# A two-layer gated decoder trunk on one core: more weight units in seven products, softmax every three steps, the residual in device memory, ScalarE's own silu and gelu

## The chip, the cores and the metric

One core of one Trainium2 chip runs the whole program. The metric is the device time of one execution in microseconds, lower is better. The engines are named as in the profile: PE is TensorE (PEld its weight loads), DVE is VectorE, ACT is ScalarE, POOL is GpSimd, SP is SyncE, which here only issues transfers.

## The reference, cut

The input x is 256 positions of 2048 channels in float32. Two layers run one after the other; each is:

```python
h = rms_norm(x, mix_norm[l])
q, k, v, uv, gate_logits = jnp.split(h @ w_in[l], cuts, axis=-1)     # 1024 | 256 | 256 | 2048 | 4096 columns
q = apply_rope(rms_norm(q, q_norm[l])); k = apply_rope(rms_norm(k, k_norm[l]))
branch_a = sliding_window_attention(q, k, v, sinks[l]) @ w_attn_branch[l]        # window 128, blocks of 128, sinks
branch_b = chunked_sgu(gelu(uv), w_spatial[l], b_spatial[l], ...) @ w_sgu_branch[l]
gates = sigmoid(gate_logits)
x = x + (gates[..., :2048] * branch_a + gates[..., 2048:] * branch_b) @ w_out[l]
h2 = rms_norm(x, ffn_norm[l])
x = x + (silu(h2 @ w_gate[l]) * (h2 @ w_up[l])) @ w_down[l]                     # 5632 hidden channels
```

All weights and results are float32.

## The kernel before

**Products.** A float32 product is made of three matmuls in a rounded format (fp32r): the weight's high part against the activation's high part, the low part against the high, the high against the low (lines L368, L369, L370). Each weight tile is read from device memory (`raw`, 1 MB a transfer, a ring of four, SP's queue). ScalarE rounds it into `whi` (L241, six buffers, 128x1024), VectorE subtracts to get `wlo` (L249, five buffers). One such pair is a *part*. The activations are transposed, scaled and split once into `uh` and `ul`; 512 input channels of them are a *unit*.

**Jobs and units in seven.** A *job* is one product with up to 1024 output columns: a list of units, run one after the other by `run`. A plain unit has four parts of 12 matmuls. A job's first `m` units are instead made as a Strassen product of 2x2 blocks: seven parts of 6 matmuls in the order `PRODUCTS`, where four of the seven weight tiles are differences of others, made by VectorE (L224, into `sum` or in place in `raw`), and four of the activations' blocks are sums kept in `sh` and `sl` (L491, L494, L479). With m = 2 each of the seven steps does both units. `M_FFN`, `M_GATE` and the like say how many units of a job are in seven. A job in seven takes five accumulators, and ends its Strassen part with copies by ScalarE (L402, L405) and two adds by VectorE (L408).

**Order of the work.** All five engines run in the order in which the code is recorded. `stream.next` records, ahead of part i on TensorE, the high part up to i+5, the low part up to i+4 and the weight differences a little further ahead (`SUM_AHEAD`). A low part can start only when TensorE has finished the part five before, since it takes that part's buffer. Side work is put at *slots*: a plain part counts one slot, a part in seven half a slot; `after(n, fn)` records fn n slots later. `calm(n, fn)` counts plain parts alone. `evicting` takes the results of a job out of the accumulators: those of the second column half are spread over the next job, later if the next job is in seven (`T1_LATE`, `THEN_LATE`).

**Side work.** `transposed` transposes a tile by VectorE (`blk`, L454), 16 small transfers of GpSimd's queue (`tt`), a scaling and a split by ScalarE, and a subtraction by VectorE. `residual` adds a product to x, which lies in on-chip memory (`xs`), and transposes the sum for the next norm. In `Attention`, each of eight groups of heads and rows goes through `scores` (two PSUM tiles `psc`), one step later `masked`, then `exps`, `inverse`, six steps after its scores `weights` (one or two transposes `ppt`), nine after them `values` (`po`) and ten after them `weighted` (`att`, L870); groups start every `Q_STEP` steps. `psc`, `ppt`, `po` and the spatial unit's `psg` share the three PSUM buffers of the pool `ps_at`. Silu, gelu and sigmoid are built from tanh with VectorE's help, so that one activation table serves the whole program.

## Time and profile before

| | |
|---|---|
| median of 3 runs | 2468.36 us (2466.8 to 2468.55) |
| the profiled execution | 2468.03 us, its span 2466.3 us |
| busy: PE, DVE, ACT, POOL | 2455.4, 1887.3, 1373.3, 470.7 us |
| granted TensorE clock | 1.000 |
| read from device memory | 475.27 MB, 194 GB/s over the span |

A group's row in the profile gives line, engine, operation, output and inputs by the program's names, shapes and count; after the first bar the busy time and the mean of one in ns; after the second the engine's idle time just before them, and who ended most of it. A row of a timeline gives start, length, engine, line and operation, with the idle time before it in brackets. Matmuls are pipelined: one is 0.39 us long, but the next starts before it ends. VectorE's and ScalarE's operations overlap a little, too.

### The profile page before, as it was taken

How to read it: one execution, taken by the hardware profiler on the slowest of the kernel's cores; microseconds unless marked ns; L12 is line 12 of the kernel's file. 1: busy time of each engine (PE TensorE's matmuls, PEld its weight loads, DVE VectorE, ACT ScalarE, POOL GpSimd, SP SyncE). 2: the span in 40 equal slices, each digit the busy share in tenths (PEclk: the TensorE clock that was granted, in tenths of full speed). 3: DMA queues.
4: the chain of work that ended last, by engine and by line, in shares of the span. 5: the costliest groups of instructions: out<-in, count | busy, mean ns of one | idle time of the engine just before them, and what ended most of it. 6: DMA issues, size and time to landing. Idle time of an engine off the chain costs nothing.

```text
span 2466.3 us, 30726 instructions
## 1 busy us (share of the span) xinstructions
PE 2455.4 (100%) x11046; PEld 2029.3 (82%) x11046; DVE 1887.3 (77%) x2107; ACT 1373.3 (56%) x1688; POOL 470.7 (19%) x903
## 2 busy tenths in 40 slices
PE   9999999999999999999999999999999999999999
PEld 8888888888888888888888888888888888888887
DVE  6797675797977687778867976757878776977696
ACT  6565455476655555555655554544756555655554
POOL 1411300541220022002235022014402200220020
PEclk9999999999999999999999999999999999999999
DMA  8644656766565557566766456566756665665564
GB/s 295 221 156 159 213 172 221 221 217 228 204 220 190 206 204 239 171 229 199 230 235 216 156 169 207 189 195 201 252 187 239 205 208 202 206 223 189 203 205 153
DMA packets 162730, 507.73 MB, mean 206 GB/s; under 512 B 22912, under 2 KB 25584, under 8 KB 162576
## 3 DMA queue, kind: packets, MB, share of 16 engines
q1 hardware_dynamic: 134512, 477.05, 57.7%
q0 software_dynamic: 27744, 28.44, 3.8%
q8 instruction: 86, 1.41, 0.2%
q14 instruction: 68, 0.56, 0.1%
q10 hardware_dynamic: 320, 0.27, 0.0%
HBM read 475.27 MB, written 2.10 MB: 194 GB/s over the span
## 4 chain that ended last, share of the span: by engine, by line
PE 98%; DVE 1%; DMA 0%; ACT 0%; issue 0%; POOL 0%; DVEq 0%; ACTq 0%; POOLq 0%
PE acc L368 32%; PE acc L369 32%; PE acc L370 32%; PE po L864 1%; PE psc L822 1%; DMA tt<-blk 0%; PE ppt L853 0%; PE psg L949 0%; DVE wlo L249 0%; PE pt L533 0%; PE pwarm L346 0%; POOL tt L460 0%; DVE sums L491 0%; DVE blk L454 0%; DVE ul L519 0%
## 5 line engine op out<-in xcount | busy, mean ns | idle before, releaser
L249 DVE TENSOR_TENSOR wlo<-raw,whi 128x1024 fp32r<-128x1024 f32 (+1 forms) x940 | 1132.8, 1218 | 486.1 <-PE acc L369 398.1
L241 ACT ACTIVATE whi<-raw 128x1024 fp32r<-128x1024 f32 (+1 forms) x940 | 983.4, 1057 | 823.1 <-PE acc L370 746.3
L368 PE MATMUL acc<-whi,uh 128*128 128x512 f32 x3164 | 1240.0, 392 | 2.2 <-DVE gate L1043 1.5
L370 PE MATMUL acc<-whi,ul 128*128 128x512 f32 x3164 | 1233.0, 390 | 0.5 <-DVE ul L561 0.5
L369 PE MATMUL acc<-wlo,uh 128*128 128x512 f32 x3164 | 1232.8, 390 | 0.7 <-DVE wlo L249 0.7
L460 POOL DMA_DIRECT2D tt<-blk x800 | 392.2, 497 | 1715.4 <-DVE blk L454 959.7
L368 PEld LDWEIGHTS acc<-whi,uh 128*128 128x128 f32 x3164 | 594.3, 188 | 130.6 <-ACT acc L402 2.7
L370 PEld LDWEIGHTS acc<-whi,ul 128*128 128x128 f32 x3164 | 594.2, 188 | 124.9 <-DVE ul L561 1.0
L369 PEld LDWEIGHTS acc<-wlo,uh 128*128 128x128 f32 x3164 | 594.5, 188 | 122.1 <-DVE wlo L249 1.4
L368 PE MATMUL acc<-whi,sh 128*128 128x512 f32 x336 | 131.0, 390 | 0.8 <-ACT acc L402 0.8
L370 PE MATMUL acc<-whi,sl 128*128 128x512 f32 x336 | 130.9, 390 | 0.0
L369 PE MATMUL acc<-wlo,sh 128*128 128x512 f32 x336 | 130.9, 389 | 0.0
L241 ACT ACTIVATE whi<-sum 128x1024 fp32r<-128x1024 f32 x84 | 89.0, 1059 | 72.7 <-PE acc L370 56.7
L249 DVE TENSOR_TENSOR wlo<-sum,whi 128x1024 fp32r<-128x1024 f32 x84 | 102.6, 1222 | 13.4 <-ACT whi L241 11.0
L402 ACT ACTIVATE acc<-acc 128x512 f32<-128x512 f32 x126 | 74.4, 590 | 21.7 <-PE acc L370 19.8
L368 PEld LDWEIGHTS acc<-whi,sh 128*128 128x128 f32 x336 | 63.1, 188 | 14.3 <-ACT acc L402 1.2
L370 PEld LDWEIGHTS acc<-whi,sl 128*128 128x128 f32 x336 | 63.1, 188 | 13.1
L369 PEld LDWEIGHTS acc<-wlo,sh 128*128 128x128 f32 x336 | 63.1, 188 | 13.0
L561 DVE TENSOR_TENSOR ul<-tt,uh 128x1024 fp32r<-128x1024 f32 x38 | 46.5, 1223 | 34.1 <-ACT uh L558 27.3
L558 ACT ACTIVATE uh<-tt 128x1024 fp32r<-128x1024 f32 x38 | 40.2, 1057 | 43.9 <-DMA tt<-blk 41.3
L408 DVE TENSOR_TENSOR acc<-acc,p 128x512 f32<-128x512 f32 x84 | 54.2, 691 | 0.0
L224 DVE TENSOR_TENSOR sum<-raw,raw 128x1024 f32<-128x1024 f32 x42 | 51.5, 1226 | 1.4
(131 smaller groups left out, 1053.1 us busy)
## 6 DMA issues: line engine op xcount, KB each, us to landing
raw<-in_w_in_dram SPq DMA_DIRECT2D x112, 1024.0 KB, 5.1
raw<-in_w_down_dram SPq DMA_DIRECT2D x88, 1024.0 KB, 6.3
raw<-in_w_gate_dram SPq DMA_DIRECT2D x80, 1024.0 KB, 5.8
raw<-in_w_up_dram SPq DMA_DIRECT2D x80, 1024.0 KB, 5.1
raw<-in_w_out_dram SPq DMA_DIRECT2D x32, 1024.0 KB, 6.7
tt<-blk POOLq DMA_DIRECT2D x800, 32.0 KB, 5.1
raw<-in_w_attn_branch_dram SPq DMA_DIRECT2D x16, 1024.0 KB, 6.4
raw<-in_w_sgu_branch_dram SPq DMA_DIRECT2D x16, 1024.0 KB, 5.6
```

The lines of the kernel that those rows point to most:

```text
L224: nc.vector.tensor_tensor(out=self.raw(dst), in0=self.raw(total[0]), in1=self.raw(total[1]), op=ALU.subtract)
L241: nc.scalar.activation(hi[:, k, :], raw[:, k, :], AF.Copy)
L249: nc.vector.tensor_tensor(out=lo[:, k, :], in0=raw[:, k, :], in1=hi[:, k, :].bitcast(F32), op=ALU.subtract)
L368: nc.tensor.matmul(ps, a, hi, start=first, stop=False, skip_group_check=True)
L369: nc.tensor.matmul(ps, a, lo, start=False, stop=False, skip_group_check=True)
L370: nc.tensor.matmul(ps, b, hi, start=False, stop=last, skip_group_check=True)
L402: nc.scalar.activation({"11": x, "t2": e, "t3": y}[name], a, AF.Copy)
L408: nc.vector.tensor_tensor(out=d, in0=d, in1=fifth, op=ALU.add)
L460: nc.gpsimd.dma_start(blocks(d)[:, :, i] if whole else d[:, i].rearrange("p k t c -> p (k t) c"), src)
L558: nc.scalar.activation(blocks(unit.hi), tv, AF.Copy)
L561: nc.vector.tensor_tensor(out=blocks(unit.lo), in0=tv, in1=blocks(unit.hi).bitcast(F32), op=ALU.subtract)
L822: nc.tensor.matmul(pscore[:, i, :nk], self.qT[pair // 4][j * HD:(j + 1) * HD, pair % 4, t * P:(t + 1) * P], self.kT[j * HD:(j + 1) * HD, : ...
```

## The change

- *Units in seven.* In the FFN, the gate jobs of two columns blocks have m = 2 in place of 1 (five in each layer); the first of the four attention-gate jobs has m = 1 in place of 0 (one in each layer). The second unit of the FFN's norm therefore gets its sums, too, and the sums of the mixing norm's unit 0 are made earlier. `wsum` has two buffers.
- *Softmax.* `Q_STEP` is 3 in place of 4.
- *Residual.* x is read chunk by chunk (`fetch_x`, SP's queue) before a job that adds to it, and written back to device memory (`keep_x`, SP's queue) after it. The 16 KB of each partition go to three more general slots (`N_BIG`) and to `wsum`.
- *Functions.* Silu and gelu are ScalarE's own (`AF.Silu`, `AF.Gelu_apprx_tanh`). Sigmoid and softmax stay with tanh and exp.
- *Lateness.* The evictions' delays now depend on the number of units in seven of the next job.

```diff
+N_SUM = 2
-N_BIG = 24
+N_BIG = 27
-T1_LATE, THEN_LATE = 1.5, 3
+T1_LATE, THEN_LATE, UNIT_LATE = (1.5, 3), (3, 7), (3, 3)
-Q_STEP = 4
+Q_STEP = 3
-M_OUT, M_FFN, M_DOWN = (0, 1), 1, 1
+M_OUT, M_FFN, M_DOWN = (0, 1), (2, 1, 1), 1
-M_GATE, M_ATT, M_SGU = (0, 1, 1, 1), (0, 0), (0, 0)
+M_GATE, M_ATT, M_SGU = (1, 1, 1, 1), (0, 0), (0, 0)
...
+    def fetch_x(c):
+        xt[c] = slot([P, NT, CW], name="x")
+        nc.sync.dma_start(xt[c], rows(home[c]))
+
+    def keep_x(c):
+        nc.sync.dma_start(rows(kept[c]), xt[c])
+        home[c] = kept[c]
...
         def gelu(self, c, ps, dst):
-            sq = slot([P, NT, CW], name="sq")
...
+            evicting(c, lambda t: None,
+                     ahead=lambda t: nc.scalar.activation(dst[:, t, :], ps[t], AF.Gelu_apprx_tanh, scale=self.nrm.r[t]))
...
+                square_at = 5 if c == 0 else behind(2, 2, 5)
                 def then():
-                    nxt.unit(o, sums=sums and o == 0)
-                    after(5 if c == 0 else 2, lambda: nxt.squares(o))
+                    nxt.unit(o, sums=o < sums)
+                    after(square_at, lambda: nxt.squares(o))
...
-                evicting(c, lambda t: added(o, t, ps), then if nxt is not None else None)
+                evicting(c, lambda t: added(o, t, ps), then if nxt is not None else None, late_then=UNIT_LATE)
+                if out_at is None:
+                    after(2 if c == 0 else behind(3, 4), lambda: keep_x(o))
...
+            job = jobs[job_no[0]]
+            length = 3.5 * job.m + 4 * (len(job.units) - job.m)
+            after(length - 8, lambda j=j: fetch_x(j))
+            after(length - 6, lambda j=j: fetch_x(j + 1))
             run(units, done)
...
         run(norm.units, spa.v)
+        after(6, lambda nrm=norm: nrm.add_sums(0))
         run(norm.units, spa.u)
...
-                def tanh(t):
-                    nc.scalar.activation(a[:, t, :], ps[t], AF.Tanh, scale=norm.rh[t])
-
-                def gated(t):
-                    th = a[:, t, :]
-                    nc.vector.scalar_tensor_tensor(out=th, in0=th, scalar=1.0, in1=ps[t], op0=ALU.add, op1=ALU.mult)
-
-                evicting(c, gated, ahead=tanh)
+                evicting(c, lambda t: None,
+                         ahead=lambda t: nc.scalar.activation(a[:, t, :], ps[t], AF.Silu, scale=norm.r[t]))
```

The order in which the instructions then stand is shown at two places. The first is VectorE's row in the second gate job of a round of the FFN of layer 0, just after the up job before it; `wlo` are low parts, a difference of `raw` or `sum` is a weight for the Strassen product, `hid` is the eviction of the up job, `blk` its transposes. Before (one unit in seven):

```order
L249 TENSOR_TENSOR wlo_5165<-raw_5045,whi_5143 128x1024
L224 TENSOR_TENSOR raw_5045<-raw_5079,sum_5147 128x2x512
L224 TENSOR_TENSOR raw_5045<-raw_5079,raw_5045 128x2x512
L249 TENSOR_TENSOR wlo_5183<-sum_5147,whi_5163 128x1024
L224 TENSOR_TENSOR sum_5147<-raw_5079,raw_5045 128x1024
L249 TENSOR_TENSOR wlo_5200<-raw_5045,whi_5181 128x1024
L1084 SCALAR_TENSOR_TENSOR hid_4893<-acc_4934,rr_875_4813,hid_4893 128x512
L1084 SCALAR_TENSOR_TENSOR hid_4893<-acc_4936,rr_877_4817,hid_4893 128x512
L454 STREAM_TRANSPOSE blk_5221<-hid_4893 128x4x4x32 x2
L249 TENSOR_TENSOR wlo_5243<-raw_5079,whi_5198 128x1024
L249 TENSOR_TENSOR wlo_5264<-raw_5045,whi_5241 128x1024
```

After (two units in seven), from the third low of the job on:

```order
L249 TENSOR_TENSOR wlo_5223<-sum_5189,whi_5203 128x1024
L224 TENSOR_TENSOR raw_5069<-raw_5103,sum_5189 128x2x512
L1080 SCALAR_TENSOR_TENSOR hid_4921<-acc_4960,rstd_892_4831,hid_4921 128x512
L1080 SCALAR_TENSOR_TENSOR hid_4921<-acc_4962,rstd_894_4836,hid_4921 128x512
L469 STREAM_TRANSPOSE blk_5245<-hid_4921 128x4x4x32 x2
L249 TENSOR_TENSOR wlo_5267<-sum_5207,whi_5221 128x1024
L224 TENSOR_TENSOR raw_5153<-raw_5171,sum_5207 128x2x512
L249 TENSOR_TENSOR wlo_5289<-raw_5069,whi_5265 128x1024
L224 TENSOR_TENSOR raw_5069<-raw_5103,raw_5069 128x2x512
L1080 SCALAR_TENSOR_TENSOR hid_4956<-acc_4961,rstd_892_4831,hid_4956 128x512
L249 TENSOR_TENSOR wlo_5301<-raw_5153,whi_5287 128x1024
L224 TENSOR_TENSOR raw_5153<-raw_5171,raw_5153 128x2x512
```

Fourteen lows and eight differences now stand in one run, and the evictions of the up job stand among its first ones. In VectorE's row, the third low to the eleventh are nine lows, six differences, four evictions and two transposes.

The second place is TensorE's row in the softmax of layer 0, at a step where a group's scores begin; the bracket names the counters that an instruction waits for (DVE is VectorE's, Activation ScalarE's, DMASW those of transfers). Before, these tiles stand at three steps, with 12 matmuls of the stream between them and the next; here is the step of the transposes:

```order
L370 MATMUL acc_1194<-whi_1408,ul_362 128x512
L853 MATMUL ppt_1593<-ident,pr_1389 128x128 [waits DVE_49,Activation_49]
L853 MATMUL ppt_1593<-ident,pr_1389 128x128 [waits Activation_49] x3
L853 MATMUL ppt_1600<-ident,pr_1389 128x128 [waits DVE_49]
L853 MATMUL ppt_1600<-ident,pr_1389 128x128 x3
L368 MATMUL acc_1193<-whi_1437,uh_361 128x512
```

After:

```order
L834 MATMUL psc_1553<-tt_482,qT_813 128x128
L834 MATMUL psc_1556<-tt_482,qT_813 128x128 [waits DMASW6_49,DMASW3_49,DMASW7_49,DMASW2_49,DVE_49]
L834 MATMUL psc_1556<-tt_482,qT_813 128x128
L876 MATMUL po_1573<-kv_195,pT_1475 128x64 [waits Activation_49]
L876 MATMUL po_1573<-kv_195,pT_1475 128x64 x3
L865 MATMUL ppt_1578<-ident,pr_1341 128x128 [waits DVE_49]
L865 MATMUL ppt_1578<-ident,pr_1341 128x128 x3
L865 MATMUL ppt_1585<-ident,pr_1341 128x128 [waits DVE_49]
```

Scores, values and transposes now stand at one step. On VectorE, the operation that reads `po_1573`, and the one that reads `psc_1553`, stand behind the next low:

```order
L249 TENSOR_TENSOR wlo_1594<-raw_1306,whi_1530 128x1024
L224 TENSOR_TENSOR sum_1596<-raw_1369 128x1024
L882 TENSOR_TENSOR att_774<-po_1573,rd_1251 128x256
L856 TENSOR_TENSOR den_1443<-den_1443,es_1442 128x4
L857 RECIPROCAL rd_1444<-den_1443 128x4
L841 TENSOR_TENSOR pr_1548<-psc_1553,mask 128x2x128
```

That low, `wlo_1594`, takes the buffer of the part that stands ahead of the step on TensorE.

More of the change, by code (lines that the diff above doesn't have):

```diff
@@ L291, in flush, with behind, evicting @@
             coming.pop(0)()
-    def behind(whole, strassen):
-        return strassen if job_no[0] < len(jobs) and jobs[job_no[0]].m else whole
-    def evicting(c, fn, then=None, ahead=None):
+    def behind(*by_units):
+        return by_units[min(jobs[job_no[0]].m if job_no[0] < len(jobs) else 0, len(by_units) - 1)]
+    def evicting(c, fn, then=None, ahead=None, late_then=THEN_LATE):
         if c == 0 or job_no[0] == len(jobs):
@@ L306, in evicting @@
         else:
-            late = behind(1, T1_LATE)
+            late = behind(1, *T1_LATE)
             if ahead is not None:
@@ L313, in evicting @@
             if then is not None:
-                after(behind(2, THEN_LATE), then)
+                after(behind(2, *late_then), then)
     def tick(n=1, first=None):
@@ L325, in tick, with rows @@
                 fn()
-    xs = const.tile([P, NT, D], F32, name="xs")
+    xt = [slot([P, NT, CW], name="x") for _ in range(NCH)]
+    home = [x[0, :, c * CW:(c + 1) * CW] for c in range(NCH)]
+    kept = [dram.tile([S, CW], F32, name=f"kept{c}") for c in range(NCH)]
+    def rows(v):
+        return v.rearrange("(t p) n -> p t n", p=P)
+    def fetch_x(c):
[4 more added lines that the diff above has]
+        home[c] = kept[c]
     for c in range(NCH):
         for t in range(NT):
-            nc.sync.dma_start(xs[:, t, c * CW:(c + 1) * CW],
+            nc.sync.dma_start(xt[c][:, t, :],
                               x[0, t * P:(t + 1) * P, c * CW:(c + 1) * CW])
@@ L589, in squares @@
                 junk = temp(name="junk")
-                nc.scalar.activation(junk, xs[:, t, c * CW:(c + 1) * CW], AF.Square,
+                nc.scalar.activation(junk, xt[c][:, t, :], AF.Square,
                                      accum_out=self.ss[t][:, c:c + 1])
         def unit(self, c, on_pe=False, sums=False, at_once=False):
-            transposed(self.units, c, xs[:, :, c * CW:(c + 1) * CW], cols=self.cols[:, 4 * c:4 * c + 4],
+            transposed(self.units, c, xt[c], cols=self.cols[:, 4 * c:4 * c + 4],
                        on_pe=on_pe, sums=sums, at_once=at_once)
         def finish(self):
-            self.r, self.rh, self.rr = [], [], []
+            self.r, self.rh = [], []
             for t in range(NT):
@@ L1049, in merge @@
             nc.vector.tensor_tensor(out=flat(ga[j]), in0=flat(ga[j]), in1=flat(gb[j]), op=ALU.add)
-        after(2, lambda nrm=norm: nrm.add_sums(0))
         for j in (0, 2):
@@ L1083, in upped @@
                 def upped(t):
-                    nc.vector.scalar_tensor_tensor(out=a[:, t, :], in0=ps[t], scalar=norm.rr[t], in1=a[:, t, :],
+                    nc.vector.scalar_tensor_tensor(out=a[:, t, :], in0=ps[t], scalar=norm.r[t], in1=a[:, t, :],
                                                    op0=ALU.mult, op1=ALU.mult)
@@ L1099, in hybrid_trunk @@
             else:
-                residual(hT, None, False)
+                residual(hT, None, 0)
         norm = nxt
```

45 lines of the change are left out of this document (13 added, 32 removed).

## The prediction

> **What bounds the kernel now.** I read the head of the page first, then the chain that ended last, then the groups by line with their idle time, then a window of one plain stage, and last single instructions at the places that the change touches.
>
> ```profile
> span 2466.3 us, 30726 instructions
> PE 2455.4 (100%) x11046; PEld 2029.3 (82%) x11046; DVE 1887.3 (77%) x2107; ACT 1373.3 (56%) x1688; POOL 470.7 (19%) x903
> PE 98%; DVE 1%; DMA 0%; ACT 0%; issue 0%; POOL 0%; DVEq 0%; ACTq 0%; POOLq 0%
> 560.00:900.00 340.00, 340.00 (x1501) 281.45 (x1500) 267.12 (x265) 190.79 (x210) 50.19 (x103) 1.00 0.63 211
> L249 DVE TENSOR_TENSOR wlo<-raw,whi 128x1024 fp32r<-128x1024 f32 x936 | 1130.3, 1221 | 486.1 <-PE acc L369 398.1 <-issue 45.6 <-ACT whi L241 21.2
> L241 ACT ACTIVATE whi<-raw 128x1024 fp32r<-128x1024 f32 x936 | 981.3, 1059 | 823.1 <-PE acc L370 746.3 <-issue 28.6 <-DVE raw L224 12.1
> PEld acc L369 <- DVE wlo L249: 1.4, 2, 0.8
> ```
>
> TensorE is the bound: it makes 98% of the chain, and in the window of FFN work (from 560 to 900 us; the columns are stretch, length, PE, PEld, DVE, ACT, POOL, clock, DMA share, GB/s) it issues 1501 matmuls in 340.0 us, 0.2265 us each, at clock 1.00. It waited for a low part of a weight only twice, 1.4 us in all. VectorE mostly waits for TensorE to give back one of the five low buffers (398 us before L249). So the time follows the count of matmuls, as long as VectorE's lead of five parts lasts. A "part" here is one high/low pair: 12 matmuls in a plain unit (2.72 us), 6 in a product of seven (1.36 us).
>
> How long it lasts is what the change turns on, so I look at the tightest regular place of before, a w_down product in seven at 1196 to 1214 us.
>
> ```profile
> 1195.08 0.18 DVE L714 SCALAR_TENSOR_TENSOR sa<-sn,gn 128x32 f32<-128x32 f32 x1
> 1195.19 1.22 DVE L249 TENSOR_TENSOR wlo<-raw,whi 128x1024 fp32r<-128x1024 f32 x1
> 1196.44 1.23 DVE L224 TENSOR_TENSOR raw<-raw,sum 128x1024 f32<-128x1024 f32 x1
> 1197.58 1.22 DVE L224 TENSOR_TENSOR raw<-raw,raw 128x1024 f32<-128x1024 f32 x1
> ...
> 1202.25 1.28 DVE L984 TENSOR_TENSOR xs<-acc,xs 128x512 f32<-128x512 f32 x2
> 1203.44 1.29 DVE L454 STREAM_TRANSPOSE blk<-xs 128x512 f32<-128x512 f32 x2
> 1204.66 1.18 DVE L249 TENSOR_TENSOR wlo<-raw,whi 128x1024 fp32r<-128x1024 f32 x1
> ...
> 1210.37 3.49 DVE L249 TENSOR_TENSOR wlo<-raw,whi 128x1024 fp32r<-128x1024 f32 x3
> 1214.28 0.39 PE L369 MATMUL acc<-wlo,uh 128*128 128x512 f32 x1
> ```
>
> VectorE runs here without a pause: an operation on 128x1024 starts 1.14 us after the one before (1196.44, 1197.58), two adds on 128x512 take 1.2, two transposes 1.22. The first low of the last row ends at 1211.6; its first user on TensorE starts at 1214.28. The lead is down to 2.7 us. A sum gives the same: from the part that frees the first buffer to this one TensorE has five plain parts and seven of six, 23.1 us; VectorE has nine lows, four weight sums, four adds, two transposes and 18 small table rows of 0.1, 20.1 us. The 3.0 us left compare with 2.7 measured, so I use such sums for the kernel after.
>
> **The change part by part.** *Products in seven.* A unit in seven has 42 matmuls, a whole one 48. Ten gate products of the FFN and two attention gates each get one more: 72 matmuls fewer, 72 x 0.2265 = -16.3 us, all on the path. Each such unit also brings 3 more high and 3 more low parts and 4 weight sums: VectorE 7 x 1.14 = 8.0 us, ScalarE 3.2.
>
> ```profile
> L224 DVE TENSOR_TENSOR sum<-raw,raw 128x1024 f32<-128x1024 f32 x42 | 51.5, 1226 | 1.4
> L1084 DVE SCALAR_TENSOR_TENSOR hid<-acc,rr,hid 128x512 f32<-128x512 f32 x44 | 31.9, 744 | 0.0
> L1076 DVE SCALAR_TENSOR_TENSOR hid<-hid,acc 128x512 f32<-128x512 f32 x44 | 28.9, 680 | 0.0
> L893 DVE SCALAR_TENSOR_TENSOR sq<-sq,v 128x1024 f32<-128x1024 f32 x4 | 4.9, 1222 | 0.5 <-ACT v L890 0.5
> L870 DVE TENSOR_TENSOR att<-po,rd 128x256 f32<-128x256 f32 x16 | 6.6, 416 | 1.4 <-PE po L864 1.4
> L864 PE MATMUL po<-kv,pT 128*128 128x64 f32 x192 | 23.1, 270 | 0.0
> L343 ACT ACT_TABLE_LOAD x1 | 1.3, 1283 | 1.3 <-PEq L1117 1.3
> ```
>
> Over the whole span VectorE gets 12 x 8.0 = 96 us more and loses 28.9 (L1076) and 19 of gelu (16 rows like L893): about 1935 of 2450, on average no bound. Locally it is one. In a stretch of two units in seven TensorE takes 14 x 1.36 = 19 us, VectorE 14 lows and 8 sums, 25 us; only the lead covers the rest.
>
> Second gate of a round (after an up product; four of them). From the end of the part that frees the buffer of the third low to the eleventh part TensorE has two plain parts and ten of six, 19.0 us. VectorE stands in a row with nine lows and six sums (15 x 1.14 + 0.08 = 17.2), four evictions of the up product (L1084 above: 0.74 long, so 0.66 apart, 2.6) and two transposes (1.2): 21.0. It comes 2.0 us late, four times: +8.0.
>
> First gate of the FFN (one in each layer). Four plain parts and ten of six, 24.5 us, against eleven lows, eight sums, one more low of the new sums for unit 1 (22.9), four adds and four transposes (4.8), four sums of a quarter's size (as L870's, 0.34 apart, 1.4): 29.1. Late by 4.6, twice: +9.2.
>
> Gate after a w_down (four): as the second gate, with four adds of 0.6 in place of evictions and transposes, 19.6 against 19.0: 0.5 late each, +2.0.
>
> *Softmax every three steps.* A group's weights stand six steps after its scores and its values nine. With a step of four these met other groups' scores nowhere; with three all fall on one step: two score tiles, one value tile, one or two transposed weight tiles through three PSUM buffers. So the transposes (`ppt`) must take the buffer of the value tile written just before, and wait until VectorE has multiplied it into `att` (L870), which stands one step later in VectorE's row, behind the next low.
>
> ```profile
> 200.19 1.07 PE psc L822 x8
> 204.20 0.84 PE po L864 x8
> 189.70 1.73 PE po L864 x16
> 207.86 0.44 PE ppt L853 x4
> 140.00:240.00 100.00, 99.31 (x513) 81.29 (x512) 82.96 (x148) 59.20 (x118) 11.84 (x19) 1.00 0.45 146
> ```
>
> Floor: with VectorE ready, the tail of the last `po` matmul (0.27 long, 0.11 apart), the multiply (0.42) and two semaphore steps of 0.05 (at 1797.49 in the next fence TensorE follows a low that ended at 1797.44) cannot be hidden: 0.65 in five steps of a layer, 0.2 in a sixth, where other transposes stand between: 6.9 us in both layers. Ceiling: VectorE, 83% busy in this window of before, gets the same work in three quarters of the steps. From part 40 to the first such step I count 24.7 us on it against 23.4 on TensorE (seven parts, psc, ppt and po as above), so the multiply comes 1.5 us late, and as late at the next two. I take 1.5 in three steps, 0.65 in two, 0.2 in one: 6.0 in a layer, +12.0.
>
> *What leaves with before's stalls.* Before, the first FFN gate of layer 1 stood three times.
>
> ```profile
> 1768.10 0.39 PE L370 MATMUL acc<-whi,ul 128*128 128x512 f32 x1
> 1769.24 0.50 PE L368 MATMUL acc<-whi,sh 128*128 128x512 f32 x1 [0.75 <-ACT acc L402]
> 1775.90 1.29 DVE L454 STREAM_TRANSPOSE blk<-xs 128x512 f32<-128x512 f32 x2
> 1793.38 1.71 ACT L554 ACTIVATE tt<-tt,vcols 128x256 f32<-128x256 f32 x4 [4.90 <-DMA tt<-blk]
> 1795.15 0.39 PE L370 MATMUL acc<-whi,ul 128*128 128x512 f32 x1
> 1796.23 0.50 PE L368 MATMUL acc<-whi,uh 128*128 128x512 f32 x1 [0.69 <-ACT uh L558]
> 1796.21 1.23 DVE L561 TENSOR_TENSOR ul<-tt,uh 128x1024 fp32r<-128x1024 f32 x1 [5.00 <-ACT uh L558]
> 1796.57 0.40 PE L369 MATMUL acc<-wlo,uh 128*128 128x512 f32 x1
> 1797.49 0.50 PE L370 MATMUL acc<-whi,ul 128*128 128x512 f32 x1 [0.53 <-DVE ul L561]
> ```
>
> Starts 1.14, 1.08 and 0.92 apart in place of 0.23 make 2.5 us. VectorE's new lateness covers them: -2.5. But the last two came from unit 3 being transposed late: 20 us pass from the transposes (1777.2) to its low (1797.4). After the change some 17.4 us are left between the same points, the new stall counted. Between 0 and 2.8 us each, I take 1.0 in each layer: +2.0.
>
> *Residual in device memory.* 32 reads and 28 writes of 512 KB stand in SP's row; what hides them is the four-deep ring of weights. A write waits for the adds, and the weights behind it on SP wait too.
>
> ```profile
> SPq L203 <- DVE wlo L249: 1958.5, 401, 18.1
> raw<-in_w_gate_dram SPq DMA_DIRECT2D x80, 1024.0 KB, 5.8
> xs<-in_x_dram SPq DMA_DIRECT2D x8, 256.0 KB, 6.4
> ```
>
> In the first gate the fourth write stands ahead of unit 2's weights: issued after the add, landed 5.8 us later, split in 2.3, they reach TensorE between 0.6 us early and 0.4 late; zero elsewhere. I take 0.
>
> *Own silu and gelu.* One ScalarE operation replaces two or three; 14 more table loads, 14 x 1.28 = 18 us on an engine that idles 44% and waits 746 us for TensorE to return high buffers. I take 0. The Trainium skill (ScalarE: Activation LUTs, What ACT_TABLE_LOAD costs) states some 1283 ns for a load, as L343 shows, and a drain of 1380 ns beside it, which no row here shows; by that the loads take 37 us of ScalarE in place of 18, and by the same cover the sum stays.
>
> **Sum.** -16.3 + 8.0 + 9.2 + 2.0 + 12.0 - 2.5 + 2.0 = +14.4 us on a span of 2466.3. The profiled execution took 2468.03 us, 1.7 around its span, and the median of the runs is 2468.36. 2468.4 + 14.4 = 2482.8; I say 2483.
>
> **Rivals.** (1) Faster: the lead holds. If VectorE's row in the FFN stretches were 2 us shorter in the second gates and 4.6 in the first (a pitch of 0.9 us in place of 1.14 would do it, or lows that may start two parts earlier), the 19.2 us and the 2.0 of unit 3 go: 2468.4 - 16.3 + 12.0 - 2.5 = 2461.6. For it: VectorE waited 398 us for buffers and is 77% busy. Against it: the sum met the measured lead to 0.3 us, on the short side. Chance 0.13.
> (2) About level: each late place at its floor, 6.9 in softmax, the FFN sums 0.2 smaller each (the second matmul, not the first, needs the low): -16.3 + 6.9 + 17.2 - 2.5 = +5.3, or 2474. Chance 0.13.
> (3) Slower still: ScalarE enters the row. Three table loads stand between exponentials, gelu and the copies of `ppt` within some 14 parts of softmax; if these copies wait for them, and unit 3 costs its 2.8, and all weights behind a write come 0.4 late: 2 x 3 x 1.28 + 3.6 + 0.8 = 12 more, 2495. For it: in-order ScalarE; against: TensorE then waits anyway. Chance 0.14.
>
> **How the numbers follow.** The forecast has 0.60. A measurement of this kernel can tell about 0.2%, 5 us. Rival 1 is the faster case, 0.13; rival 2 lies at the edge of 5 us, most of it within, 0.12; the rest, 0.75, is slower. The range takes in rivals 2 and 3 with their edges, 2468 to 2498, and leaves rival 1 out.
>
> **What would show it.** Right: 72 matmuls fewer on the three lines; waits of `ppt` for `att` on PE, six in a layer, some 1 us; PE waiting for the low line in ten gate products, 0.5 to 5 us each. Wrong: if PE waits for lows under 5 us in all, the lead is misjudged (rival 1); if `ppt` waits are 0.65 everywhere, VectorE was not behind (rival 2); if PE waits on ScalarE's copies, rival 3.

## Result, and the profile after

The changed kernel takes 2574.71 us (median of 4 runs, 2574.09 to 2576.03), the kernel before 2467.58 beside it: a ratio of 1.0435, 95% interval 1.0417 to 1.0453. It is 107 us slower; the forecast was 15 slower, with 2498 as its upper end. The head of the page after (span, busy time by engine, shares of the chain that ended last):

```profile
span 2573.2 us, 30862 instructions
PE 2484.1 (97%) x10974; PEld 2032.4 (79%) x10974; DVE 1941.7 (75%) x2137; ACT 1413.3 (55%) x1724; POOL 471.0 (18%) x903
PE 88%; DVE 5%; DMA 3%; issue 2%; ACT 2%; SPq 0%; POOL 0%; DVEq 0%; ACTq 0%; POOLq 0%
```

The 72 matmuls did go (11046 to 10974), but TensorE is busy for 2484 us in place of 2455 and makes 88% of the chain in place of 98%. Fewer matmuls and more busy time together mean that some of them ran slower. Its waits (engine, line, what it waited for, us in total, times, longest), and one of ScalarE's:

```profile
PE acc L383 <- ACT acc L417: 35.2, 17, 4.1
PE ppt L865 <- DVE att L882: 17.5, 11, 4.0
PE acc L384 <- DVE wlo L249: 10.5, 16, 2.1
PE pf L363 <- DMA first_rows<-in_mix_norm_dram: 10.4, 1, 10.4
PE acc L383 <- DVE x L982: 2.7, 1, 2.7
...
ACT whi L241 <- DMA raw<-in_w_gate_dram: 89.9, 32, 7.1
```

The second row is the forecast's softmax wait and the third its wait for low parts. The first, the fourth, the fifth and ScalarE's were in no term of the sum. A table from the trace shows where the 106.9 us of span went. Each product's length is taken from its first matmul to that of the next, before and after, and the matmuls that it no longer has (0.2265 us each) stand in a row of their own:

| part | forecast, us | in the trace after, us |
|---|---|---|
| 72 matmuls fewer | -16.3 | -16.3 |
| start, up to the first product (8.6 before, 19.6 after) | 0 | +11.0 |
| product u and first attention gate, both layers (111.3 before; 125.7 and 127.2) | +12.0 | +33.0 |
| first FFN gates, 2 | +8.7 (9.2 + 2.0 - 2.5) | +32.7 |
| FFN gates after a w_down, 4 | +2.0 | +27.4 |
| second FFN gates, 4 | +8.0 | +8.4 |
| up products, 10 | 0 | +5.6 |
| layer 1's q product | 0 | +4.6 |
| the rest | 0 | +0.6 |

Three of these places are read here; the first FFN gates, whose excess has several parts, are taken up in experiments 2 and 9. At the start (first rows of before, then of after; the row at 4.08 is one of the chain that ended last):

```profile
0.80 0.42 ACTq L337 DMA_DIRECT2D first_rows<-in_mix_norm_dram  x1
8.62 0.47 PE L368 MATMUL acc<-whi,uh 128*128 128x512 f32 x1
...
4.08 6.09 DMA x<-in_x_dram
10.19 0.39 ACTq L352 DMA_DIRECT2D first_rows<-in_mix_norm_dram  x1
10.62 1.28 ACT L358 ACT_TABLE_LOAD   x1 [10.62 <-DMA x<-in_x_dram]
19.63 0.48 PE L383 MATMUL acc<-whi,uh 128*128 128x512 f32 x1
```

An 8 KB transfer is issued at 10.19 us in place of 0.80, after a wait for a transfer of x, with which it has nothing to do. In the program it now stands behind the transfers of x and of the first weights. The trace shows eight completion counters that the transfers take in turn; this one takes the counter of the eighth transfer, issued at 4.08, and so it waits until that one has landed at 10.17.

In a gate after a w_down (after; SP's rows are DMA issues, whose time is from the first of a row to the last):

```profile
846.81 0.68 DVE L982 TENSOR_TENSOR x<-acc,x 128x512 f32<-128x512 f32 x1
...
832.70 15.18 SPq L341 DMA_DIRECT2D kept<-x  x2
847.98 2.35 SPq L203 DMA_DIRECT2D raw<-in_w_gate_dram  x4
...
845.87 1.06 ACT L241 ACTIVATE whi<-sum 128x1024 fp32r<-128x1024 f32 x1
853.79 1.06 ACT L241 ACTIVATE whi<-raw 128x1024 fp32r<-128x1024 f32 x1 [6.85 <-DMA raw<-in_w_gate_dram]
854.75 0.58 ACT L417 ACTIVATE acc<-acc 128x512 f32<-128x512 f32 x1
...
851.08 0.39 PE L385 MATMUL acc<-whi,sl 128*128 128x512 f32 x1
855.39 0.80 PE L383 MATMUL acc<-whi,uh 128*128 128x512 f32 x1 [3.92 <-ACT acc L417]
855.98 0.63 PE L384 MATMUL acc<-wlo,uh 128*128 128x512 f32 x1
...
855.00:858.30 3.30, 2.91 (x7) 2.34 (x8) 3.07 (x4) 3.28 (x4) 0.00 (x0) 0.50 1.03 421
```

Read it upwards. TensorE stands 3.9 us for a copy on ScalarE (L417). That copy stands in ScalarE's row behind a high part, which waits 6.85 us for weights. The weights were issued at 847.98, since two writes of the residual stood ahead of them on SP, the second of which waited for an add on VectorE (first row) that ended at 847.49. And when TensorE goes on, the granted clock is 0.50 for 3.3 us (last row; the clock is the number after POOL's, and 7 matmuls start in it): at half clock a matmul starts every 0.43 us and not every 0.23.

In softmax (the rows with a long wait in layer 0 after; then product u after and before, where the clock again is the number after POOL's):

```profile
164.46 1.11 PE L865 MATMUL ppt<-ident,pr 128*128 128x128 f32 x4 [3.95 <-DVE att L882]
179.09 2.01 PE L865 MATMUL ppt<-ident,pr 128*128 128x128 f32 x8 [2.02 <-DVE att L882]
194.46 1.25 PE L865 MATMUL ppt<-ident,pr 128*128 128x128 f32 x8 [1.87 <-DVE att L882]
...
133.90:201.00 67.10, 59.25 (x289) 47.73 (x288) 55.76 (x119) 35.51 (x75) 8.01 (x7) 0.92 0.32 109
...
123.40:176.80 53.40, 53.40 (x274) 43.39 (x272) 48.89 (x107) 33.89 (x70) 7.63 (x7) 1.00 0.47 157
```

The waits are where the forecast had them, but 2 to 4 us long. Clock 0.92 over 67.1 us is up to another 5.4 us (0.90 over 68.1, 6.8, in layer 1); it is less by what of the half clock falls into the waits themselves.

### The profile page after: what moved, and what is told of

It is laid out like the page before. It is cut to its first block, busy times and chain, and to the rows that moved or that the text cites. A ratio compares the mean times of both kernels' runs of the same rounds, so it can differ in the third digit from the quotient of the medians.

```text
span 2573.2 us, 30862 instructions
## 1 busy us (share of the span) xinstructions
PE 2484.1 (97%) x10974; PEld 2032.4 (79%) x10974; DVE 1941.7 (75%) x2137; ACT 1413.3 (55%) x1724; POOL 471.0 (18%) x903
## 4 chain that ended last, share of the span: by engine, by line
PE 88%; DVE 5%; DMA 3%; issue 2%; ACT 2%; SPq 0%; POOL 0%; DVEq 0%; ACTq 0%; POOLq 0%
PE acc L383 29%; PE acc L384 29%; PE acc L385 28%; DVE wlo L249 2%; DMA tt<-blk 1%; DMA raw<-in_w_gate_dram 1%; ACT whi L241 1%; PE ppt L865 1%; DVE sum L224 1%; PE po L876 0%; ACT acc L417 0%; PE psc L834 0%; DVE ul L576 0%; DMA x<-in_x_dram 0%; PE pt L548 0%
## 5 line engine op out<-in xcount | busy, mean ns | idle before, releaser
L383 PE MATMUL acc<-whi,uh 128*128 128x512 f32 x3044 | 1200.6, 394 | 26.7 <-ACT acc L417 22.6
L385 PE MATMUL acc<-whi,ul 128*128 128x512 f32 x3044 | 1193.5, 392 | 4.4 <-DVE ul L576 4.4
L384 PE MATMUL acc<-wlo,uh 128*128 128x512 f32 x3044 | 1193.9, 392 | 0.8 <-DVE wlo L249 0.8
L383 PE MATMUL acc<-whi,sh 128*128 128x512 f32 x432 | 171.0, 396 | 13.0 <-ACT acc L417 12.6
L384 PE MATMUL acc<-wlo,sh 128*128 128x512 f32 x432 | 172.1, 398 | 10.6 <-DVE wlo L249 9.8
L385 PE MATMUL acc<-whi,sl 128*128 128x512 f32 x432 | 169.4, 392 | 0.0
L241 ACT ACTIVATE whi<-sum 128x1024 fp32r<-128x1024 f32 x108 | 114.5, 1060 | 92.1 <-PE acc L385 49.7
L249 DVE TENSOR_TENSOR wlo<-sum,whi 128x1024 fp32r<-128x1024 f32 x108 | 130.7, 1218 | 23.2 <-ACT whi L241 18.6
L417 ACT ACTIVATE acc<-acc 128x512 f32<-128x512 f32 x132 | 77.5, 587 | 14.8 <-PE acc L385 13.7
L224 DVE TENSOR_TENSOR raw<-raw,sum 128x1024 f32<-128x1024 f32 x54 | 66.0, 1221 | 1.2
L224 DVE TENSOR_TENSOR sum<-raw 128x1024 f32<-128x1024 f32 x54 | 65.8, 1219 | 0.0
```

Of the source, the lines that this page charges most:

```text
L224: nc.vector.tensor_tensor(out=self.raw(dst), in0=self.raw(total[0]), in1=self.raw(total[1]), op=ALU.subtract)
L241: nc.scalar.activation(hi[:, k, :], raw[:, k, :], AF.Copy)
L249: nc.vector.tensor_tensor(out=lo[:, k, :], in0=raw[:, k, :], in1=hi[:, k, :].bitcast(F32), op=ALU.subtract)
L383: nc.tensor.matmul(ps, a, hi, start=first, stop=False, skip_group_check=True)
L384: nc.tensor.matmul(ps, a, lo, start=False, stop=False, skip_group_check=True)
L385: nc.tensor.matmul(ps, b, hi, start=False, stop=last, skip_group_check=True)
```

## Experiments

All times are medians of the kernel, beside the kernel before, which took 2467.2 to 2467.7; a number like 1.0388 is the ratio to it.

**1. The start alone.** One transfer moved ahead of the loop over x:

```diff
+    first_rows = slot([16, P], name="first_rows")
+    nc.scalar.dma_start(first_rows, mix_norm[0]...)
     for c in range(NCH):
         for t in range(NT):
             nc.sync.dma_start(xt[c][:, t, :], ...)
-    first_rows = slot([16, P], name="first_rows")
-    nc.scalar.dma_start(first_rows, mix_norm[0]...)
```

> The changed kernel with one line moved: the transfer of first_rows is written ahead of the eight transfers of x. Nothing is left out. Theory A (the start costs by itself): in the trace after, this transfer was issued at 10.19 us, when an x transfer had landed, and the first matmul of a product started at 19.6 us against 8.6 before; with the line moved it starts near 8.6 and the time falls by about 11 us, to 2564. Rival B (the start waits for x and the first weights in any case, first_rows only shows it): under 2 us.

2564.39 us, ratio 1.0388 (1.0371 to 1.0406): 10.3 less than the changed kernel, theory A. The first matmul of a product starts at 8.16 us.

**2. The residual's write behind the weights.**

```diff
-                    after(2 if c == 0 else behind(3, 4), lambda: keep_x(o))
+                    after(2 if c == 0 else behind(3, 4, 9), lambda: keep_x(o))
```

> The changed kernel, in which the write of the second output's residual (keep_x) comes nine steps after the product in place of four where that product has two units in seven: on SP it then stands behind the weights of units 2 and 3 and not ahead of them, in six gates. Theory A (the write makes the weights late: in the gate at 834 us SP stood at the writes until 847.98, the weights landed at 853.8, TensorE stood 4.1 us and ran at half clock for 2.6 more): the weights of unit 2 go out at about 844.6, when their buffers come free, 3.4 us earlier; four gates after w_down lose about 5.5 us each and the two first gates 4 to 6 each, 30 to 34 us in all, 2541 to 2545. Rival B (four raw buffers held by two units in seven make the weights late, with or without the write): under 10 us, and ScalarE's high parts still wait for raw.

2543.49 us, 1.0310 (1.0294 to 1.0325): 31.2 less, theory A. The same gate, now with SP's, ScalarE's and the whole gate's rows:

```profile
844.38 5.51 SPq L203 DMA_DIRECT2D raw<-in_w_gate_dram  x4
857.94 0.46 SPq L341 DMA_DIRECT2D kept<-x  x1
...
849.45 1.06 ACT L241 ACTIVATE whi<-raw 128x1024 fp32r<-128x1024 f32 x1 [2.78 <-DMA raw<-in_w_gate_dram]
...
834.00:876.00 42.00, 41.94 (x184) 34.03 (x183) 37.80 (x36) 26.68 (x30) 0.00 (x0) 1.00 0.61 219
```

The weights go out 3.6 us earlier, ScalarE still waits for them, but TensorE does not wait for ScalarE and the clock stays at 1.00. By the measure of the table above, the four gates after a w_down now cost 0.55 to 0.63 us each, 2.3 in all, where the forecast had 2.0. So four buffers held by two units are tight, but cost no more than these 0.6 us by themselves; a write that waits in front of the weights does. The first gates fall from 32.7 to 25.3 us, and TensorE's waits for ScalarE's copies (L417) from 35.2 to 12.7.

**3. Softmax every four steps.**

```diff
-Q_STEP = 3
+Q_STEP = 4
-M_GATE, M_ATT, M_SGU = (1, 1, 1, 1), (0, 0), (0, 0)
+M_GATE, M_ATT, M_SGU = (0, 1, 1, 1), (0, 0), (0, 0)
```

> The changed kernel with softmax every four steps and the first attention gate in whole products again (with a step of four this gate has to be whole, or the attention isn't ready in time). Theory A (the coinciding softmax steps cost 8.9 us of waits in each layer, and the halved clock behind them another 5 to 7): the products u and first attention gate come back from 125.7 and 127.2 us to 111.3 in each layer, about 30 us less, 2544; the granted clock in u is 1.00. Rival B (as forecast, 6.0 us a layer, and the rest comes from elsewhere): 12.0 less 2.7 for the matmuls, 9 us less, 2565.

2542.98 us, 1.0310 (1.0295 to 1.0325): 31.7 less, theory A. Product u is at 53.3 us and clock 1.00, u and first gate together at 111.3, as before the change. The edit takes back the denser softmax and the first gate in seven together; experiment 8 parts the steps from the rest.

**4. FFN gates with one unit in seven.**

```diff
-M_OUT, M_FFN, M_DOWN = (0, 1), (2, 1, 1), 1
+M_OUT, M_FFN, M_DOWN = (0, 1), (1, 1, 1), 1
```

> The changed kernel with the FFN gates at one unit in seven, as before the change; the residual still goes through device memory and silu and gelu are own functions. Theory A (late weights and a late VectorE in gates with two units make up the FFN's excess: 32.7 us in first gates, 27.4 in those after w_down, 8.4 in second ones, 5 in up products, less 13.6 for 60 matmuls): about 60 us less, 2515, and no wait for raw. Rival B (the residual's transfers cost by themselves, whichever product follows): 7 us or more stay in each place where a write stands, 40 us less or fewer, 2535.

2519.96 us, 1.0211 (1.0196 to 1.0226): 54.8 less, nearer to A. What it leaves are 3.2 and 2.2 us in the first gates (over their length before) and 4.0 in layer 1's q.

**5. These three together** (edits 1, 3 and 4).

> The changed kernel with three parts undone together: first_rows is fetched ahead of x, softmax every four steps with the first attention gate whole, FFN gates at one unit in seven. What is left of the change is the residual in device memory and the own silu and gelu. Theory A (the parts add up: 10.3, 31.7 and 54.8 us in the runs that undid one each): 2574.7 - 96.8 = 2478, with some 4 us left in layer 1's q product and 2 to 3 in each first gate. Theory B (what stayed in those runs was an after-effect of the other parts): 2468, level with the kernel before.

2477.64 us, 1.0040 (1.0025 to 1.0055): theory A's 2478 to 0.4 us, so the three parts add up. 10 us are left, and in them the residual's transfers and the own functions.

**6. The residual back in SBUF** (edit 5, with `fetch_x` and `keep_x` empty):

```diff
-    xt = [slot([P, NT, CW], name="x") for _ in range(NCH)]
+    xt = [const.tile([P, NT, CW], F32, name=f"x{c}") for c in range(NCH)]
-N_SUM = 2
+N_SUM = 1
-N_BIG = 27
+N_BIG = 24
```

> As a5_undone, and the residual stays in SBUF (four tiles of its own, no reads or writes of it; 24 slots and one sum buffer, as before the change). So only silu and gelu are new. Theory A (the residual's transfers, on SP and beside the transposes' transfers, cost what is left in a5_undone): 2465 to 2468. Theory B (the table loads and the order on ScalarE cost it): the same time as a5_undone, near 2478.

2468.21 us, 1.0001 (0.9992 to 1.0011): theory A. With softmax every four steps, own silu and gelu with their table loads make no difference that can be measured, and the residual's transfers cost 9.4 us even where no product has two units. One mechanism of this shows in the changed kernel at layer 1's q, where the chunks are transposed through small transfers (POOL). The windows with these transfers, before and after (the last two columns are the DMA share and GB/s):

```profile
1222.00:1235.00 13.00, 13.00 (x59) 10.78 (x58) 9.66 (x11) 11.67 (x18) 3.79 (x8) 1.00 0.86 290
...
1277.00:1290.00 13.00, 13.00 (x59) 10.77 (x58) 7.46 (x8) 7.38 (x13) 4.81 (x10) 1.00 1.03 364
```

With reads and writes of x between the weights the DMA engines have no room left; the last small transfers land later, VectorE stands for them with the adds of the last output behind, and TensorE waits 2.7 us for the adds (L982 in the list of waits above). That the DMA share is the cause is argued from these rows; no run changed it alone.

**7. Two units in the up products and not in the gates** (edit 5, edit 2, which moves no write when the gates have one unit, and):

```diff
-M_OUT, M_FFN, M_DOWN = (0, 1), (1, 1, 1), 1
+M_OUT, M_FFN, M_DOWN = (0, 1), (1, 2, 1), 1
```

> As a5_undone, but ten up products of the FFN have two units in seven in place of the gates, and a second write of the residual would stand behind the weights. Ahead of an up product stands a gate, which with its own silu is evicted by ScalarE alone. Theory A (VectorE's sum for the second gates without the eviction and the transposes: nine lows and six weight sums, 17.2 us, against TensorE's 19.0): no waits, 60 matmuls fewer, 13.6 us under a5_undone. Theory B (a pair of units costs by its buffers: four raw buffers and five low ones held): each product waits about 2 us as the second gates did, 0.6 us net, a5_undone + 6.

2469.93 us, 1.0007 (0.9998 to 1.0017): 7.7 under experiment 5 and not 13.6, between the theories and nearer to A. The up products themselves behave as theory A has it. One of them, from first to last matmul:

```profile
838.00:878.80 40.80, 40.80 (x182) 33.78 (x181) 38.30 (x37) 25.13 (x27) 0.67 (x2) 1.00 0.57 206
```

180 matmuls take 40.77 us; all ten up products take 40.80, with VectorE 94% busy. What is lost again lies in the first gates (6.0 us and 6.7 over their matmuls; 3.7 and 4.3 in experiment 5) and in layer 1's q (4.3 over its length before; 2.5 in experiment 5). The first gates have to make the second unit's sums in the row of the residual's adds.

**8. Scores, weights and values on steps of their own**, still every three steps:

```diff
-            for n, step in ((1, masked), (2, exps), (4, inverse), (6, weights), (9, values), (10, weighted)):
+            for n, step in ((1, masked), (2, exps), (4, inverse), (7, weights), (11, values), (12, weighted)):
```

> The changed kernel, softmax still every three steps, with a group's transposed weights seven steps after its scores in place of six, its values eleven in place of nine and their product one step later: scores, weights and values of three groups then fall on three different steps, and the weights take buffers of scores that VectorE has masked. Theory A (the steps coincide, and the weights take the buffer just written by the values): the waits of ppt for att, 8.9 us a layer, and the half clock behind them, 5 to 7, go: 25 us less, 2550, with step three kept. Theory B (VectorE, with the same softmax work in three quarters of the steps, is behind whatever the offsets): the waits move to other lines, under 8 us less.

2555.26 us, 1.0354 (1.0338 to 1.0369): 19.4 less, between the theories and nearer to A; its four runs lie between 2547.2 and 2559.1, so this figure is good to some 6 us. The waits of `ppt` for `att` fall from 17.5 us to 4.8, 2.9 for ScalarE's copies come in, and u with the first gate takes 115.6 and 117.5 us; 4.2 us in layer 0 and 6.1 in layer 1 over the old length stay, though this version has six matmuls fewer there. So some 19 of the 33.0 us are the coincidence of the steps. The rest is put down to the denser softmax; no run tested that alone.

**9. The gates without the residual's transfers** (edit 6, and):

```diff
-M_OUT, M_FFN, M_DOWN = (0, 1), (1, 1, 1), 1
+M_OUT, M_FFN, M_DOWN = (0, 1), (2, 1, 1), 1
-N_SUM = 1
+N_SUM = 2
-N_BIG = 24
+N_BIG = 23
```

> a8_sbuf (residual in SBUF, own silu and gelu, softmax every four steps) with the FFN gates of two units in seven as the changed kernel has them, in 23 slots. No residual is written or read, so this measures the products alone. Theory A (the forecast's own terms: 60 matmuls fewer 13.6, second gates 8.0, first gates 9.2 with 2.0 for unit 3, gates after w_down 2.0): 2468.2 - 13.6 + 21.2 = 2476. Theory B (the first gates cost by themselves what they still cost in a2_keep, 13.3 and 12.0 us over the ideal): 2468.2 - 13.6 + 8.4 + 2.3 + 25.3 = 2491.

2492.11 us, 1.0101 (1.0084 to 1.0118): theory B. Against experiment 6 that is 23.9 us more. Second gates cost 8.3 us, those after a w_down 2.4, as forecast; the two first gates cost 20 more than in experiment 6, and up products 4.2. TensorE's rows with a wait in layer 0's first gate up to 570 us, and the row of VectorE that ends the last one:

```profile
546.57 0.50 PE L380 MATMUL acc<-whi,sh 128*128 128x512 f32 x1 [1.07 <-ACT acc L414]
550.24 0.50 PE L381 MATMUL acc<-wlo,uh 128*128 128x512 f32 x1 [0.43 <-DVE wlo L249]
553.64 0.50 PE L381 MATMUL acc<-wlo,sh 128*128 128x512 f32 x1 [0.40 <-DVE wlo L249]
555.91 0.50 PE L381 MATMUL acc<-wlo,sh 128*128 128x512 f32 x1 [0.62 <-DVE wlo L249]
558.83 0.51 PE L381 MATMUL acc<-wlo,sh 128*128 128x512 f32 x1 [1.26 <-DVE wlo L249]
567.98 0.50 PE L382 MATMUL acc<-whi,ul 128*128 128x512 f32 x1 [3.17 <-DVE ul L573]
...
566.71 1.22 DVE L573 TENSOR_TENSOR ul<-tt,uh 128x1024 fp32r<-128x1024 f32 x1
```

The first five waits make 3.8 us, with the slow restarts behind them 5.1: the forecast had 4.6. Of the 5.1, though, 1.3 belong to the first row, a copy by ScalarE that the forecast had not; VectorE's lows make 3.8. And VectorE runs on without a pause until the low of unit 2's data (`ul`), which TensorE needs next; TensorE waits another 3.2 us for it and 0.3 for unit 3's, 4.0 with restarts, and 1.6 go to half clock.

**10. The whole change with three repairs** (edits 1, 2 and 8).

> The whole change with three repairs together: first_rows fetched first, the second write of the residual behind the weights, softmax's weights and values on steps of their own (as a1_start, a2_keep, s1_spread). Theory A (the three are apart): 2574.7 - 10.3 - 31.2 - 19.4 = 2514. Theory B (they share stalls and half clock): 2525 or more.

2511.18 us, 1.0174 (1.0159 to 1.0190): theory A to 3 us. The gains of the three repairs add up.

**11. Halts of TensorE made on purpose** in the kernel before:

```diff
+            if n == 0:
+                idle = temp(name="idle") if job_no[0] - 1 in EXTRA else None
+                if idle is not None:
+                    nc.vector.memset(idle, 0.0)
+                for _ in range(EXTRA.get(job_no[0] - 1, 0)):
+                    nc.vector.tensor_tensor(out=idle, in0=idle, in1=idle, op=ALU.subtract)
```

> The kernel before, with extra subtractions of zeros on a spare tile (128x512, about 0.6 us each) in VectorE's row at the start of eight plain products, the two attention and the two sgu branches of each layer: 22, 26, 20, 24 in layer 0 and 28, 23, 30, 21 in layer 1. They change no result; TensorE, which runs five parts ahead, is to stand there between 0 and some 7 us. Theory A (as the trace after reads: a window of 3.41 us in which TensorE idles more than about half of it is followed by 3.41 us at half clock): every stall over about 2 us that falls into one window is followed by 0.43 us per matmul for 3.4 us, 1.7 us more. Theory B (only an idle time of a whole window or more, 3.4 us, halves the clock): stalls of 2 to 3.4 us leave the clock at 1.00.

A single run took 2558.2 us. The halts were longer than aimed at, 2.3 to 11.8 us; one of 2.84 us, of which no window held more than 2.24, did halve the clock, against theory B. So the same with fewer subtractions:

> As c1_stalls, where the shortest halt was 2.85 us and all of them halved the clock, with fewer subtractions: 15, 17, 16, 18 in layer 0 and 17, 19, 16, 18 in layer 1, for halts of TensorE between 0.5 and 3 us. Theory A (half clock after a window of 3.41 us with about half of it idle): halts under 1.5 us, and longer ones split over two windows, leave the clock at 1.00; those of 2 us and over within one window halve it for 3.4 us. Theory B (any halt that drains TensorE halves it): halts of 0.5 to 1.5 us do too.

This took 2512.1 us in a single run, with halts of 2.1 to 5.3 us; none was as short as the 0.5 to 1.5 us of theory B. Two halts, and the clock behind each:

```profile
324.24 0.80 PE L370 MATMUL acc<-wlo,uh 128*128 128x512 f32 x1 [2.54 <-DVE wlo L250]
478.23 0.50 PE L369 MATMUL acc<-whi,uh 128*128 128x512 f32 x1 [2.10 <-DVE gate L1050]
...
324.30:327.00 2.70, 2.70 (x7) 2.12 (x8) 2.70 (x3) 0.00 (x0) 0.00 (x0) 0.50 0.29 26
478.30:481.60 3.30, 3.30 (x15) 2.69 (x16) 2.74 (x3) 0.00 (x0) 1.97 (x4) 1.00 0.94 292
```

The trace's clock records change only at multiples of 3.41 us from one another. Set against these windows, the halts of both kernels under 3.9 us read:

| halt, us | idle in each window that it touches | clock in the window after each |
|---|---|---|
| 2.10 | 1.13, 0.96 | 1.00, 1.00 |
| 2.29 | 0.97, 1.32 | 1.00, 1.00 |
| 2.39 | 2.39 | 0.50 |
| 2.54 | 1.97, 0.58 | 0.50, 1.00 |
| 2.84 | 2.24, 0.60 | 0.50, 0.50 |
| 2.86 | 0.28, 2.58 | 1.00, 0.50 |
| 3.53 | 0.98, 2.55 | 1.00, 0.50 |
| 3.84 | 1.45, 2.39 | 1.00, 0.50 |

Theory A: up to 1.45 us of idle in a window at full clock left the clock alone, 1.97 and more halved it in the next; and theory B of the second run falls with the halts of 2.10 and 2.29 us. Where the limit lies between 1.45 and 1.97 was not tried. In the other traces windows with 1.2 to 1.9 us idle fell on both sides.

**12. What the runs point to**: the residual in SBUF, softmax every four steps, up products with two units, the moved transfer of experiment 1, and the second unit's sums made later. Own silu and gelu stay. Beside the values of experiments 3, 6 and 7, with slots and sum buffers as in experiment 9:

```diff
-        residual(mT, norm, max(M_FFN), scale=0.5)
+        residual(mT, norm, 1, scale=0.5)
...
+            if i == 0:
+                after(10, lambda nrm=norm: nrm.add_sums(1))
```

> What the runs point to: own silu and gelu, the residual in SBUF (23 slots and two sum buffers), softmax every four steps, gates in products of one unit, and the ten up products with two units in seven; the second unit's sums are made ten steps into the first FFN gate (as add_sums does for unit 0 of the other norm) and not in the row of the residual's adds. Theory A (a8_sbuf less 60 matmuls of 0.2265 us, since a6_up2 showed no wait in an up product, and the first gates as in a8_sbuf): 2468.2 - 13.6 = 2455, 0.5% under the kernel before. Theory B (one slot fewer and two more of them held for the sums make transposes and hidden rows late): 2460 to 2468.

2457.99 us, 0.9962 (0.9950 to 0.9975): 10.2 under experiment 6 in place of 13.6, between the theories. Second sums now cost 1.7 and 1.9 us in the first up products, and one wait of 0.9 came up in layer 1's q. One more gate with two units, behind a gate that ScalarE alone evicts:

```diff
-M_GATE, M_ATT, M_SGU = (0, 1, 1, 1), (0, 0), (0, 0)
+M_GATE, M_ATT, M_SGU = (0, 1, 1, 2), (0, 0), (0, 0)
...
+        after(8, lambda nrm=norm: nrm.add_sums(1))
         for j in (0, 2):
             gate(gb, j)
```

> f1_sbuf_up2, and the last gate of the second branch (gb, columns 2 and 3) with two units in seven as well; ahead of it stands a gate whose tanh is on ScalarE alone. Theory A (same rule: no eviction by VectorE ahead of it, so no wait): 12 matmuls fewer, 2.7 us under f1_sbuf_up2. Theory B (the adds for unit 1's sums, about 3 us of VectorE, and the longer hold of two more slots cost what is won): level with f1_sbuf_up2 or above.

2454.03 us, 0.9947 (0.9933 to 0.9961): faster than both kernels, 13.1 us under the one before. Its page:

```profile
span 2454.8 us, 30686 instructions
PE 2441.6 (99%) x10974; PEld 2014.5 (82%) x10974; DVE 1947.3 (79%) x2147; ACT 1408.8 (57%) x1714; POOL 469.2 (19%) x903
PE 93%; DMA 3%; DVE 2%; issue 1%; POOL 1%; ACT 1%; DVEq 0%; ACTq 0%; POOLq 0%
```

It has the 10974 matmuls of the changed kernel, and VectorE is as busy (1947 us against 1942). Where the two-unit products stand decides what they are worth: with the residual in SBUF, the 60 matmuls saved in the up products gave 10.2 us (f1_sbuf_up2 against experiment 6), and the same number saved in the gates lost 23.9 (experiment 9 against 6). The gain of f3_gb2 over f1_sbuf_up2, 4.0 us for a forecast of 2.7, is not told apart from 2.7: the runs of the two span 2 and 3.5 us.

## Why the prediction was wrong, step by step

The direction held: the matmuls saved are outweighed by waits. As the parts add up (experiment 5), either of two named terms would have carried it: softmax (31.7 us, experiment 3) or the FFN gates (23.9, experiment 9). The size missed by 92 us, and the runs say where: the residual 40.6 for 0, softmax 31.7 for 9.3, the FFN gates 23.9 for 5.1 (18.7 of waits less 13.6 of matmuls), and the start 10.3 for 0.

- **The residual, taken as 0.** This is the step that failed most. The prediction saw that a write waits for the adds and the weights behind it wait too, gave the first gate "between 0.6 us early and 0.4 late" and wrote "zero elsewhere". Moving the write behind the weights is worth 31.2 us (experiment 2), and the transfers themselves another 9.4 (experiment 6 against 5). The cover named, a ring of four weights, is gone exactly where a product has two units, since these hold all four; and the second output's add comes late there, since the change itself set it to three steps (T1_LATE). That the lateness of the add has this share in it is read from the program; no run changed it alone. Two parts of the change were each costed at their old surroundings.
- **The start, not looked at.** 10.3 us (experiment 1) from the order of one 8 KB transfer. The prediction took the stages one by one and left the start out, though this transfer had moved behind those of x in the program and taken a counter that was in use.
- **Softmax, +12.0.** Place and reason of the waits were right, and their number nearly (5 and 6 for 6 a layer). Taken were 1.5 us where VectorE is behind, though the counts behind it, 24.7 less 23.4, give 1.3; found were 1.9 to 4.0, 8.9 and 8.6 a layer for 6.0. The ceiling was worked out at the first step and used for the others. Up to 5.4 and 6.8 us of half clock and 2.5 a layer for ScalarE's copies in the first attention gate came on top: 31.7 measured for 9.3 (12.0 less 2.7 of matmuls).
- **The price of a halt.** The sum took every halt at its length. A halt of some 2 us in one window costs 1.7 more (experiment 11), and the first matmul behind it some tenths (855.39 to 855.98 above, 0.59 apart). The granted clock of the whole span fell from 1.000 to 0.984. After the start, the clock record of the changed kernel stands at half for 20 windows, 68.3 us, of which TensorE idles 8.8; half of the rest, some 30 of the 107 us, is an estimate of what the clock added. It is contained in the sums above. The prediction's fences showed the column at 1.00 everywhere, and it never asked what would move it.
- **VectorE's row in seven-products: half right.** Second gates +8.0, measured 8.4; gates after a w_down +2.0, measured 2.3 once the write is out of the way. First gates +4.6 each: measured 5.1 for the parts counted (1.3 of it ScalarE's copy), then 4.0 for the lows of units 2 and 3 (1.0 was taken), then 1.6 of half clock, which is 10 a gate more than in experiment 6 (experiment 9). By the measure of the table, both first gates together cost 32.7 us in the changed kernel, 25.3 with the write moved and 19.5 with the residual in SBUF, against 8.7 forecast. The count ended at the eleventh part, while VectorE's row, and the debt in it, went on.
- **Own silu and gelu at 0:** right with softmax every four steps (experiment 6). The 14 loads took 1.28 us each, and in each case the load started 0.02 to 0.34 us after the end of the operation before it and the next operation 1.3 us after the load's start. With three steps, one load (at 205.07 us in layer 0) stands four operations ahead of a copy for which TensorE waits 1.3 us; no run tells its share there. That their evictions leave VectorE, and so decide where a two-unit product is free, was not seen; it is what experiments 7 and 12 live on.

Of the rivals, the third named the wait that came, TensorE on ScalarE's copies, 35.2 us, but mostly not its reason: these were the products' own copies, 22.5 us of them gone when the weights came in time (experiment 2), and not `ppt`'s behind table loads.

## What to carry to other kernels

Before calling a transfer hidden, name the buffer that covers it and ask whether another part of the same change holds that buffer; and look on an in-order queue for what a waiting write keeps back. Put more work on a busy engine only behind a stage that leaves that engine free: the same two-unit product cost 2 us behind a VectorE eviction and nothing behind a ScalarE one. Price a halt of the bounding engine with its clock, and read the order of the first ten transfers as closely as the inner loop.

## What the runs showed of the hardware

In experiment 11 TensorE's clock went by windows of 3.41 us: 1.97 us of idle time in one halved it in the next, 2.29 spread over two (0.97 and 1.32) did not. At half clock less idle time was enough to stay there: after 0.60 to 2.4 us idle in a half-clock window of these two runs the next was at half clock too, after 0.44 and 0.58 it was not. The Trainium skill (TensorE: Matmul & The Clock Gate, HAM oscillation — how this bites in real kernels) gives as its rule no idle gaps over about 3.4 us. The window's length agrees with these traces, the rule doesn't: gaps of 2.4 to 2.9 us were enough here, and the measurement decides.

A high part on ScalarE that waits for weights holds up copies that have nothing to do with them: TensorE's waits for a 0.58 us copy made 35.2 us, and 12.7 once the weights were issued earlier (experiment 2).
